# A hybrid encoder layer on one core: the first blocks, the token blocks and the convolution issue in written order, the conditioning is formed by quarters of the channels, h is made without GpSimd, and the staging tiles are fixed

## The chip, the cores and the metric

The kernel runs on one core of a Trainium2 chip. The metric is the device time of one execution in microseconds (us). The engines are TensorE (PE; its weight loads are listed apart as PEld), VectorE (DVE), ScalarE (ACT), GpSimd (POOL) and SyncE (SP, which here only issues transfers). Each engine works through a queue of its own in order. Transfers are issued from the queues of SP, ACT and POOL and run on 16 DMA engines.

## The reference

One layer with 2048 tokens of 1024 channels, all in float32:

```python
c_act = silu(c)
shift, scale, gate = split(c_act @ w_ada + b_ada, 3)      # the conditioning
h = rmsnorm(x, norm_w) * (1 + scale) + shift
proj = h @ w_in + b_in       # na_q, na_k, na_v, na_z, ml_q, ml_k, ml_v, ml_o, ml_z (512 columns each), 16 gate columns
na  = neighbourhood_attention(na_q, na_k, na_v, rpb) * silu(na_z)      # 32 x 64 grid, windows of 8 x 16, bias table rpb
mq, mk = silu(short_conv(ml_q, ml_k))                                  # 5 taps over the tokens
ml  = groupnorm((mlstm(mq, mk, ml_v) + mlstm_backward(...)) * sigmoid(ml_o)) * silu(ml_z)
out = rmsnorm(x + gate * (concat(na, ml) @ w_out), final_norm_w)
```

## The kernel before, in words

The product of two float32 matrices is made of three faster products: each operand is split into a high part (rounded) and a low part (the rest), and PE adds high x high, high x low and low x high. So h is kept as `hhi` and `hlo`, and a weight block as `whi` and `wlo`. A weight block is 256 columns of `w_in`; two slots, a and b, hold the block in use and the next one. A block comes in two halves (`raw0`, `raw1`); ACT copies a half into the high part and GpSimd subtracts for the low one (`load_w`).

The program runs in this order.

- **Start** (`start`). x comes in 16 tiles of 128 tokens, four to a group g (0 to 3). `prep_x` squares the four tiles on ACT, takes the reciprocal root on DVE (for group 0 on GpSimd) and scales the tiles. The conditioning is formed on DVE: for shift and scale, each of the eight row tiles of `w_ada` is multiplied by a column of silu(c) and added to `acc`, 512 columns at a time (`ada_tile`); PE then adds over the partitions with a column of ones (`columns`), and the results `gT` (scale) and `shT` (shift) are one number per channel. PE turns x into channel order (`turned`), and ACT and GpSimd, or ACT, DVE and GpSimd, make `hhi` and `hlo` for each of the eight channel tiles k (`first_h`, `scaled` and `shifted`, `make_h`).
- **Token blocks 0 and 1** (`vo_group`): values and output gate of two mLSTM heads, interleaved with the making of h for groups 1 to 3. A group is four token tiles of 24 matmuls each. In `vo_first` the four tiles are done side by side, so that they can begin when the first channels of h are there. Each result leaves PSUM (four tiles `pp`) by a DVE addition of the bias into a staging tile (`stvo`), ACT takes the sigmoid of the gate columns, and the tile is stored to `d_ck`. There are two staging tiles in turn. A store is put aside (`defer`) and issued on SP's queue when the next group ends (`flush`).
- **Token blocks 2 to 5** (`tok_blocks`): the other two heads, and the attention's values (`nav_group`, staging tile `stv`, stored to `d_vna`). Beside them runs a chain of small steps, one per token tile: the gate sums (`gate_chain`), then 16 groups of decays (`decays`): rows of `d_mneg` are loaded into one of two tiles `dec`, GpSimd adds a mask, ACT takes eight exponentials, and the result is stored to `d_ck`. Table entries for the attention's bias are filled (`table_fills`) and then spread by small DRAM to DRAM transfers (`tables_columns`, 48 of them, and `tables_rows`, 72).
- **Convolution** (`conv_blocks`): four blocks with the channels on the partitions, 32 tiles of 24 matmuls with 512 columns (`pc`); DVE does the five taps, ACT the SiLU (`acc`), and the keys are also turned by PE (`kt`) and stored through the staging tiles (`stk`).
- **Behind that**: the mLSTM passes, beside which the remaining projections run (`pq`), and the attention with the output projection.

Before the change the order of the instructions on each engine up to the attention is set by a scheduler, which takes a program order and moves instructions by estimated costs; only the attention is under `with tc.manual_schedule():`, in which instructions are issued as written. `rsqrt` is three Newton rounds of four operations (three where it is one column) behind two integer operations.

Of the kernel before, what the change touches and what calls it, by code (L numbers as in the profile page):

```python
# [15 lines left out]
P = 128  # L16
D = 1024
# [41 lines left out]
class Kernel:  # L59
# [73 lines left out]
    def phase1(self):  # L133
# [12 lines left out]
        self.stages = [self.qst, self.pool(r1a, "stage", bufs=1, side="right")]  # L146
# [17 lines left out]
        self.start(left)  # L164
        xs.close()

        self.tok_blocks(self.pool(toks, "chain", bufs=1, side="right"))
        toks.close()

        cvs = ExitStack()  # L170
        cvp = self.pool(cvs, "cvp", bufs=1, side="right")
        self.conv_blocks(cvp)
        cvs.close()
# [6 lines left out]
    def stage_tile(self, name):  # L180
        self.stages.reverse()
        return self.stages[1].tile([P, 1032], F32, tag="st", name=name).rearrange("p (o c) -> p o c", o=4)

    def load_w(self, blk, slot, halves=(0, 1)):
        nc = self.nc
        hi, lo = self.wslot[slot]
        for half in halves:
            raw = self.raw.tile([P, 4, 256], F32, tag=f"raw{half}", name=f"raw_{blk}_{half}")
            nc.sync.dma_start(raw, self.w_main[blk, :, 4 * half : 4 * half + 4, :])
            ks = slice(4 * half, 4 * half + 4)  # L190
            nc.scalar.activation(hi[:, ks, :256], raw, AF.Copy)
            nc.gpsimd.tensor_tensor(lo[:, ks, :256], raw, hi[:, ks, :256].bitcast(F32), ALU.subtract)

    def start(self, left):
        nc = self.nc
# [9 lines left out]
        xt = {}  # L205

        def load_x(tt):
            pool = early if tt // 4 == 2 else xp
            t = pool.tile([P, D], F32, tag="x", bufs=4, name=f"x_{tt}")
            nc.sync.dma_start(t, self.x[tt * P : (tt + 1) * P, :])  # L210
            xt[tt] = t

        def prep_x(tts):
            n = len(tts)
            ssq = xp.tile([P, n], F32, tag=f"ssq{n}", bufs=2, name=f"ssq_{tts[0]}")
            rst = xp.tile([P, n], F32, tag=f"rst{n}", bufs=2, name=f"rst_{tts[0]}")
            for i, tt in enumerate(tts):
                junk = xp.tile([P, D], mybir.dt.bfloat16, tag="junk", bufs=1, name=f"junk_{tt}")
                nc.scalar.activation(junk, xt[tt], AF.Square, accum_out=ssq[:, i : i + 1])
            nc.vector.tensor_scalar(ssq, ssq, 1.0 / D, EPS, ALU.mult, ALU.add)  # L220
            self.rsqrt(xp, rst, ssq, f"x{tts[0]}", nc.gpsimd if tts[0] == 0 else None)
            for i, tt in enumerate(tts):
                if tt < 4:
                    nc.scalar.activation(xt[tt], xt[tt], AF.Copy, scale=rst[:, i : i + 1])
                else:
                    nc.vector.tensor_scalar(xt[tt], xt[tt], rst[:, i : i + 1], None, ALU.mult)

        def ada_tile(part, q, kt):
            w = ada.tile([P, GT], F32, tag="wada", bufs=7, name=f"wada_{part}_{q}_{kt}")
            c0 = part * D + q * GT  # L230
            nc.sync.dma_start(w, self.w_ada[kt * P : (kt + 1) * P, c0 : c0 + GT])
            a = acc[:, c0 : c0 + GT]
            if kt == 0:
                nc.vector.tensor_scalar(a, w, cact[:, kt : kt + 1], None, ALU.mult)
            else:
                nc.vector.scalar_tensor_tensor(a, w, cact[:, kt : kt + 1], a, ALU.mult, ALU.add)
# [53 lines left out]
        for tt in range(4):  # L290
            load_x(tt)
# [1330 lines left out]
```

## Time and profile before

| | |
|---|---|
| times of three runs | 1407.24, 1409.82, 1413.92 us, median 1409.82 |
| the profiled execution | 1409.69 us, span 1407.8 us, mean granted clock 0.983 |
| PE busy | 1316.7 us (94%), 8052 matmuls |
| DVE busy | 834.7 us (59%) |
| ACT busy | 529.7 us (38%) |
| GpSimd busy | 284.5 us (20%) |
| DMA | 264.7 MB, 188 GB/s on average |

A line of a group names the source line, the engine, the operation, out<-in, the shapes, the count, and behind the bar the busy time in us, the mean of one in ns, the idle time of the engine before it and what ended that. A line of the timeline begins with start and duration in us. A line of a stretch has its bounds, its length, the busy us of PE, PEld, DVE, ACT and POOL with their instruction counts, the granted TensorE clock, the DMA share and GB/s. A line of waits is who waited, for whom, us in total, how often, and the longest. A busy PE is not a PE at its peak, since a slower clock counts as busy.

### The profile page before, as it was taken

How to read it: one execution, taken by the hardware profiler on the slowest of the kernel's cores; microseconds unless marked ns; L12 is line 12 of the kernel's file. 1: busy time of each engine (PE TensorE's matmuls, PEld its weight loads, DVE VectorE, ACT ScalarE, POOL GpSimd, SP SyncE). 2: the span in 40 equal slices, each digit the busy share in tenths (PEclk: the TensorE clock that was granted, in tenths of full speed). 3: DMA queues.
4: the chain of work that ended last, by engine and by line, in shares of the span. 5: the costliest groups of instructions: out<-in, count | busy, mean ns of one | idle time of the engine just before them, and what ended most of it. 6: DMA issues, size and time to landing. Idle time of an engine off the chain costs nothing. (4 is left out here: it accounts for less than half of the span.)

```text
span 1407.8 us, 23381 instructions
## 1 busy us (share of the span) xinstructions
PE 1316.7 (94%) x8052; PEld 1127.7 (80%) x8052; DVE 834.7 (59%) x2565; ACT 529.7 (38%) x1131; POOL 284.5 (20%) x309
## 2 busy tenths in 40 slices
PE   3989998898999999999999998999989999999996
PEld 2889998888887787788878786788867888888885
DVE  6683423211355569156757777877637777777674
ACT  4642344523222323113323313323336555555551
POOL 4353221424101010001212002212112211112111
PEclk9999999999999999999999999999999999999998
DMA  9798448777467675555666777946598897776862
GB/s 319 225 297 202 121 125 213 190 184 204 117 116 208 143 186 163 161 166 150 196 190 212 238 225 214 232 127 180 145 275 223 197 222 169 197 192 173 190 159 75
DMA packets 273036, 264.73 MB, mean 188 GB/s; under 512 B 33498, under 2 KB 233818, under 8 KB 272918
## 3 DMA queue, kind: packets, MB, share of 16 engines
q1 hardware_dynamic: 181486, 187.17, 50.3%
q0 software_dynamic: 21408, 38.05, 11.0%
q10 hardware_dynamic: 70024, 38.02, 9.6%
q8 instruction: 64, 1.05, 0.3%
q14 instruction: 54, 0.44, 0.1%
HBM read 178.62 MB, written 92.72 MB: 193 GB/s over the span
## 5 line engine op out<-in xcount | busy, mean ns | idle before, releaser
L861 PE MATMUL pq<-hhi,whi_a 128*128 128x512 f32 x512 | 211.6, 413 | 0.8 <-ACT u L769 0.8
L861 PE MATMUL pq<-hhi,wlo_a 128*128 128x512 f32 x512 | 211.4, 413 | 0.3 <-DVE wlo_a L838 0.3
L861 PE MATMUL pq<-hlo,whi_a 128*128 128x512 f32 x512 | 211.3, 413 | 0.0
L1342 ACT ACTIVATE pbuf<-pbuf,mn 128x480 f32<-128x480 f32 (+5 forms) x128 | 76.4, 598 | 115.3 <-DVE mn L1341 108.9
L861 PEld LDWEIGHTS pq<-hhi,whi_a 128*128 128x128 f32 x512 | 98.3, 192 | 19.4 <-ACT u L769 1.2
L861 PEld LDWEIGHTS pq<-hhi,wlo_a 128*128 128x128 f32 x512 | 98.2, 192 | 19.0 <-DVE wlo_a L838 0.8
L861 PEld LDWEIGHTS pq<-hlo,whi_a 128*128 128x128 f32 x512 | 98.3, 192 | 17.9
L1341 DVE CUSTOM_DVE_ANT_0 pbuf<-pS,tab 128x480 f32<-128x480 f32 (+5 forms) x128 | 65.2, 541 | 37.3 <-DMA tab<-d_t 20.1
L1415 PE MATMUL y<-hhi,whi_a 128*128 128x512 f32 x256 | 84.7, 400 | 0.7 <-ACT whi_a L1388 0.7
L1415 PE MATMUL y<-hhi,wlo_a 128*128 128x512 f32 x256 | 84.3, 399 | 0.0
L835 POOL TENSOR_TENSOR wlo_a<-rawq,whi_a 128x1024 fp32r<-128x1024 f32 x20 | 48.3, 2417 | 167.0 <-ACT whi_a L834 52.4
L425 PE MATMUL pvo<-whi_b,hhi 128*128 128x256 f32 x256 | 74.7, 292 | 7.5 <-DVE stvo L495 7.5
L1106 POOL TENSOR_TENSOR hm<-hm,ck 128x128 f32<-128x128 f32 x64 | 26.4, 413 | 266.5 <-DVE hm L1105 190.7
L1087 ACT ACTIVATE num<-px,gtile 128x129 f32<-128x129 f32 x120 | 38.2, 364 | 96.8 <-PE px L1082 79.9
L426 PE MATMUL pvo<-wlo_b,hhi 128*128 128x256 f32 x256 | 73.7, 288 | 0.0
L427 PE MATMUL pvo<-whi_b,hlo 128*128 128x256 f32 x256 | 73.5, 287 | 0.0
L1014 DVE TENSOR_SCALAR wv<-kv,gtile 128x129 f32<-128x129 f32 x120 | 38.5, 328 | 58.4 <-PE dc L1030 30.4
L495 DVE TENSOR_TENSOR stvo<-pvo,brow 128x256 f32<-128x256 f32 x64 | 26.6, 421 | 73.4 <-PE pvo L427 59.5
L710 ACT ACTIVATE dec<-dec,gtile 128x128 f32<-128x128 f32 x128 | 42.1, 392 | 74.0 <-POOL dec L706 64.8
L460 DVE TENSOR_TENSOR stv<-pv,brow 128x256 f32<-128x256 f32 x32 | 12.5, 421 | 89.2 <-DMA d_vna<-stv 41.6
L1363 PE MATMUL pT<-ident,pbuf 128*128 128x128 f32 (+2 forms) x416 | 59.8, 283 | 2.8 <-DVE pbuf L1353 2.8
L1378 PE MATMUL pO<-pt,v 128*64 128x128 f32 (+3 forms) x832 | 61.0, 280 | 1.3 <-ACT pt L1365 0.8
(295 smaller groups left out, 3578.0 us busy)
## 6 DMA issues: line engine op xcount, KB each, us to landing
ck<-d_ck SPq DMA_DIRECT2D x64, 384.5 KB
kv<-d_ck SPq DMA_DIRECT2D x120, 128.5 KB
rawq<-in_w_main_dram SPq DMA_DIRECT2D x30, 512.0 KB
raw<-in_w_main_dram SPq DMA_DIRECT2D x20, 512.0 KB
d_ck<-stvo SPq DMA_DIRECT2D x16, 514.0 KB
x<-in_x_dram SPq DMA_DIRECT2D x16, 512.0 KB
wada<-in_w_ada_dram SPq DMA_DIRECT2D x32, 256.0 KB
dec<-d_mneg SPq DMA_DIRECT2D x32, 256.0 KB
```

The costliest lines, as they stand in the source:

```text
L425: nc.tensor.matmul(ps, lhi(k), rhi(k), start=(k == 0), stop=False)
L426: nc.tensor.matmul(ps, lhi(k), rlo(k), start=False, stop=False)
L427: nc.tensor.matmul(ps, llo(k), rhi(k), start=False, stop=(k == KT - 1))
L710: nc.scalar.activation(t[:, d, o, :], t[:, d, o, :], AF.Exp, bias=self.cols["g"][:, d, h, c : c + 1])
L835: nc.gpsimd.tensor_tensor(lo[:, :, cs], raw, hi[:, :, cs].bitcast(F32), ALU.subtract)
L861: nc.tensor.matmul(patch_ps(ps) if patch else ps, w, self.htok(h, g, k, patch), start=(k == 0 and n == 0), stop=(k == KT - 1 and n == 2))
L1014: nc.vector.tensor_scalar(wv, tiles[d, i][:, 128:257], self.cols["w"][:, d, h, c : c + 1], None, ALU.mult)
L1341: nc.vector.tensor_tensor_reduce(pt[:, :nk], ps, tabs[place[u]][j][:, :nk], 1.0, 3e38, ALU.add, ALU.min, mn)
L1342: nc.scalar.activation(pt[:, :nk], pt[:, :nk], AF.Exp, bias=mn, scale=-1.0, accum_out=sums[:, j : j + 1])
L1363: nc.tensor.transpose(ps[:cs, i, :], pts[j][:, i * cs : (i + 1) * cs], self.ident)
L1378: nc.tensor.matmul(po[j * HD : (j + 1) * HD, :], v[:n, h * HD : (h + 1) * HD], pt[j][:n, i, :], start=(i == 0), stop=(i == nch - 1))
L1415: nc.tensor.matmul(y, m[:, k, :], w[k][:, cs], start=(k == 4 and n == 0), stop=(k == 3 and n == 2))
```

## The change

Everything from the start to the end of the convolution is put under the manual schedule, so the order is the written one, and the written order is changed with it. The conditioning is formed in quarters of 256 channels: for each quarter scale, then shift, then the two channel tiles of h, then their matmuls side by side. h is made by ACT (scaled, then high part) and DVE (low part); the root is taken on DVE for every group. Block 1's first group is also done side by side. The two staging tiles are made once, with their column of ones written once. Stores of the values and of the convolution go out on ACT's queue at once, those of `d_vna` on SP's; decay loads, table columns and table rows go to GpSimd's queue, the last two a few at a time. Weight halves are loaded and split at given places. The square root has one operation less in each round. The core of the diff:

```diff
-        self.stages = [self.qst, self.pool(r1a, "stage", bufs=1, side="right")]
+        stage = self.pool(r1a, "stage", bufs=1, side="right")
+        self.stages = [pl.tile([P, 1032], F32, tag="st", name=f"st{i}").rearrange("p (o c) -> p o c", o=4) for i, pl in enumerate((self.qst, stage))]
+        for st in self.stages:
+            nc.gpsimd.memset(st[:, :, 128:129], 1.0)
...
-        self.start(left)
...
+        with tc.manual_schedule():
+            self.start(left)
...
+            self.tok_blocks(self.pool(toks, "chain", bufs=1, side="right"))
...
+            self.conv_blocks(cvp)
...
+        def make_h(g, k):
+            turned(g, k)
+            scaled(g, k)
+            shifted(g, k)
...
+        def modulation(part, q):
+            c0 = part * D + q * 256
+            a = acc[:, c0 : c0 + 256]
+            for j in range(4):
+                n = 8 * q + 4 * (1 - part) + j
+                w = wada.pop(n)
+                for i in range(2):
+                    c = cact[:, 2 * j + i : 2 * j + i + 1]
+                    if j == 0 and i == 0:
+                        nc.vector.tensor_scalar(a, w[:, i, :], c, None, ALU.mult)
+                    else:
+                        nc.vector.scalar_tensor_tensor(a, w[:, i, :], c, a, ALU.mult, ALU.add)
+                load_ada(n + 7)
+            ps = self.sp.tile([P, 2], F32, tag="sp", name=f"mod_{part}_{q}")
+            for j in range(2):
+                nc.tensor.matmul(ps[:, j : j + 1], a[:, j * P : (j + 1) * P], self.ones[:, 0:1], start=True, stop=True)
...
+        prep_x(0)
+        for k in range(3):
+            turned(0, k)
+        first = self.side_by_side(0, 0)
+        for q in range(4):
...
+            modulation(1, q)
+            for k in (2 * q, 2 * q + 1):
+                scaled(0, k)
+                if k + 3 < KT:
+                    turned(0, k + 3)
...
+            modulation(0, q)
+            for k in (2 * q, 2 * q + 1):
+                shifted(0, k)
+                next(first)
...
+        self.vo_tiles(0, 0)
+        second = self.side_by_side(1, 0)
+        for k in range(KT):
+            if k == 3:
+                prep_x(1)
+            next(second)
...
+        self.chain = steps(2, ((0, 1, 2), (3, 4, 5), (6, 7)), lambda: prep_x(2))
+        self.vo_group(1, 1, 1)
...
-        self.flush()
-        dst = self.d_vna[g * GT : (g + 1) * GT, c0 : c0 + 256].rearrange("(o p) c -> p o c", p=P)
-        self.defer(lambda: nc.sync.dma_start(dst, st[:, :, :256]))
+        nc.sync.dma_start(self.d_vna[g * GT : (g + 1) * GT, c0 : c0 + 256].rearrange("(o p) c -> p o c", p=P), st[:, :, :256])
...
+    def vo_store(self, h, g):
+        nc, st = self.nc, self.stages[1]
+        nc.scalar.activation(st[:, :, 129:257], st[:, :, 129:257], AF.Sigmoid)
+        nc.scalar.dma_start(self.d_ck[h, 4 * g : 4 * g + 4, :, 128:385].rearrange("o p c -> p o c"), st[:, :, 0:257])
...
-            nc.sync.dma_start(self.d_e[ct][:, i, :, start - k0 : start - k0 + 16], self.d_rneg[:, :, dx : dx + 16])
+            self.nc.gpsimd.dma_start(self.d_e[ct][:, i, :, start - k0 : start - k0 + 16], self.d_rneg[:, :, dx : dx + 16])
+            yield
...
+        columns = itertools.chain(*(self.tables_columns(ct) for ct in range(3)))
+        self.chain = self.beside(self.chain, columns)
...
+                if g < 2:
+                    self.split_w(raws[g], (blk + 1) % 2, g)
+                next(self.fills, None)
...
-                nc.sync.dma_start(flat[:, d * 512 : (d + 1) * 512], src.broadcast_to([P, 512]))
+                nc.gpsimd.dma_start(flat[:, d * 512 : (d + 1) * 512], src.broadcast_to([P, 512]))
...
             nc.gpsimd.tensor_tensor(t, t, mask.unsqueeze(2).broadcast_to([P, 2, 4, CH]), ALU.add)
+            if n + 1 < len(groups):
+                load(n + 1)
+            yield
...
+                    for _ in range(3):
+                        next(rows, None)  
...
-        nc.sync.dma_start(dst, acc.rearrange("p (c t) -> p c t", t=CH))
+        nc.scalar.dma_start(dst, acc.rearrange("p (c t) -> p c t", t=CH))
...
-            eng.tensor_scalar(t, t, -0.5, 1.5, ALU.mult, ALU.add)
-            eng.tensor_tensor(y, y, t, ALU.mult)
+            nc.vector.scalar_tensor_tensor(y, t, 1.5, y, ALU.add, ALU.mult)
```

How the order moves is shown at three places. The first is DVE's queue in the first block, before: `acc` are the conditioning steps with 512 columns, `ssq` and `rst` belong to the root of group 0.

```order
L234 TENSOR_SCALAR acc<-wada_0_0_197,cact 128x512
L220 TENSOR_SCALAR ssq_167<-ssq_167 128x4
L1182 TENSOR_SCALAR rst_168<-ssq_167 128x4
L1183 TENSOR_SCALAR rst_168<-rst_168 128x4
L236 SCALAR_TENSOR_TENSOR acc<-wada_0_1_200,cact,acc 128x512
L236 SCALAR_TENSOR_TENSOR acc<-wada_0_2_203,cact,acc 128x512
```

The steps run on from there, all 32, and the small operations of the root are on GpSimd. Now DVE's queue from the first scale (`gT`) to the second quarter; `mod` is what PE has added over the partitions, `hlo` the low part of h for the channel tiles 0 and 1:

```order
L294 SCALAR_TENSOR_TENSOR gT<-mod_0_256,bada 128x2
L295 TENSOR_TENSOR gT<-gT,nw 128x2
L285 TENSOR_SCALAR acc<-wada_0_0_187,cact 128x256
L287 SCALAR_TENSOR_TENSOR acc<-wada_0_0_187,cact,acc 128x256
L287 SCALAR_TENSOR_TENSOR acc<-wada_0_1_189,cact,acc 128x256 x2
L287 SCALAR_TENSOR_TENSOR acc<-wada_0_2_191,cact,acc 128x256 x2
L287 SCALAR_TENSOR_TENSOR acc<-wada_0_3_242,cact,acc 128x256 x2
L297 TENSOR_TENSOR shT<-mod_0_291,bada 128x2
L251 SCALAR_TENSOR_TENSOR hlo_105<-hg_0_261,shT,hhi_102 128x512
L251 SCALAR_TENSOR_TENSOR hlo_105<-hg_1_268,shT,hhi_102 128x512
L285 TENSOR_SCALAR acc<-wada_1_0_246,cact 128x256
```

The steps of a quarter now stand behind operations that wait for PE (`gT`, `shT`) and for ACT (`hlo`).

The second place is ACT's queue where the x tiles of group 2 are squared (`junk`), before; `stvo_0_597` is the staging tile of group 1 of one block, `hhi_103` the high part of h for group 1, `hhi_104` that for group 2.

```order
L499 ACTIVATE stvo_0_597<-stvo_0_597 128x4x128
L285 ACTIVATE hhi_103<-tp_6_713,shT,gT 128x512
L285 ACTIVATE hhi_103<-tp_7_722,shT,gT 128x512
L219 ACTIVATE junk_1213,ssq_1211<-x_1095 128x1024
L219 ACTIVATE junk_1215,ssq_1211<-x_1097 128x1024
L219 ACTIVATE junk_1217,ssq_1211<-x_1099 128x1024
L219 ACTIVATE junk_1219,ssq_1211<-x_1101 128x1024
L285 ACTIVATE hhi_104<-tp_0_907,shT,gT 128x512
L285 ACTIVATE hhi_104<-tp_1_916,shT,gT 128x512
L499 ACTIVATE stvo_1_867<-stvo_1_867 128x4x128
```

And now; `st_123` is the fixed staging tile with group 1 of block 0:

```order
L493 ACTIVATE st_123<-st_123 128x4x128
L494 DMA d_ck<-st_123 128x4x257
L229 ACTIVATE junk_0_949,ssq_947<-x_572 128x1024
L229 ACTIVATE junk_1_951,ssq_947<-x_574 128x1024
L229 ACTIVATE junk_2_953,ssq_947<-x_576 128x1024
L229 ACTIVATE junk_3_955,ssq_947<-x_578 128x1024
L234 ACTIVATE x_574<-x_574,rst_948 128x1024
L234 ACTIVATE x_578<-x_578,rst_948 128x1024
L245 ACTIVATE hg_0_1006<-tp_0_1001,gT 128x512
L250 ACTIVATE hhi_104<-hg_0_1006,shT 128x512
```

The sigmoid of block 0's group 1 moved from behind the squares of group 2, where the next sigmoid stood, to ahead of them, and two of the four x tiles are now scaled by ACT behind them.

The third place is SP's queue in block 4, before: `stv` are the staging tiles, `dec` the decay rows, `d_t` table rows.

```order
L189 DMA raw_1_3278<-in_w_main_dram 128x1024
L547 DMA d_t_75<-d_e_72 8x16x192
L698 DMA dec_0_2969<-d_mneg 128x512 x2
L464 DMA d_vna<-stv_0_2752 128x4x256
L698 DMA dec_1_3064<-d_mneg 128x512 x2
L547 DMA d_t_75<-d_e_72 8x16x192 x2
L464 DMA d_vna<-stv_1_2877 128x4x256
L698 DMA dec_2_3159<-d_mneg 128x512 x2
L698 DMA dec_3_3254<-d_mneg 128x512 x2
```

And now, SP's queue at the same stores (`wide` are rows for the output gate's sums):

```order
L469 DMA brow_138<-in_b_row_dram 128x256
L401 DMA wide<-in_w_ada_dram 128x1024 x2
L466 DMA d_vna<-st_123 128x4x256
L401 DMA wide<-in_w_ada_dram 128x1024
L466 DMA d_vna<-st_124 128x4x256
L466 DMA d_vna<-st_123 128x4x256
L415 DMA wide<-in_b_gate_dram 1x1024
L466 DMA d_vna<-st_124 128x4x256
```

The decay loads and the table transfers left SP's queue, and a store stands at the end of its own group.

More of the change, by code (lines that the diff above doesn't have):

```diff
@@ L204, in start @@
         nw = ada.tile([P, KT], F32, name="nw")
[L205 to L219, printed above, removed]
+        rg = xp.tile([P, KT, 16], F32, name="rg")
```

375 lines of the change are left out of this document (170 added, 205 removed).

## The prediction

> **What bounds the kernel now.** I read the busy shares first (PE works 1316.7 of 1407.8 us), then one table of stretches, then PE's waits in the part that the change rewrites. The stretches are cut at the first transpose, the ends of the first block of matmuls, of both first weight blocks, of weight blocks 2 to 5, and of the convolution; all behind 556.9 is left as it is but for the square root. The table's columns are busy us (and instructions) of the five engines, the granted clock, and the DMA engines.
>
> ```profile
> 0.00:18.70 18.70, 0.00 (x0) 0.00 (x0) 6.87 (x15) 7.27 (x12) 6.83 (x21) 1.00 0.91 331
> 18.70:53.30 34.60, 27.90 (x160) 25.83 (x161) 27.66 (x34) 18.34 (x28) 20.08 (x16) 0.95 0.73 238
> 53.30:155.80 102.50, 96.39 (x772) 94.16 (x771) 57.15 (x131) 42.03 (x62) 37.48 (x35) 0.98 0.92 235
> 155.80:362.90 207.10, 193.18 (x1557) 189.49 (x1556) 48.31 (x112) 80.67 (x169) 58.50 (x33) 0.97 0.69 175
> 362.90:556.90 194.00, 187.86 (x833) 151.18 (x831) 118.62 (x227) 56.29 (x85) 20.02 (x8) 0.99 0.65 158
> 556.90:1407.80 850.90, 811.39 (x4736) 667.02 (x4736) 576.13 (x2051) 325.13 (x778) 141.56 (x197) 0.99 0.70 187
> ```
>
> PE is idle 18.7, 6.7, 6.1, 13.9, 6.1 and 39.5 us there. So the rewritten part can give back some 50 us at most, and only where its order doesn't bring waits of its own. Who ended those waits (us in total, times, longest), up to 600 us:
>
> ```profile
> PE tp L258 <- ACT x L224: 18.7, 1, 18.7
> PE pvo L425 <- DVE stvo L495: 7.5, 3, 3.6
> PE pv L425 <- DVE stv L460: 6.4, 2, 4.7
> PE kt L815 <- ACT acc_k L805: 6.1, 5, 2.8
> PE tp L283 <- DVE h L287: 4.6, 4, 2.1
> PE pvo L478 <- ACT hhi L265: 4.4, 1, 4.4
> ```
>
> The 13.9 us of blocks 2 to 5 are DVE's additions into the staging tile, which came late. The next lines tell why: DVE waited for the store of that tile, and the store stood on SP's queue behind loads of decay rows that waited for their buffer.
>
> ```profile
> DVE stv L460 <- DMA d_vna<-stv: 41.6, 4, 15.1
> SPq L698 <- DMA d_ck<-dec: 64.9, 18, 9.1
> ```
>
> **Term 1, the first block (to 53.3 us).** x is squared as before; the last sum is there at 10.04. The square root leaves GpSimd for DVE: 13 small operations instead of 15, 0.20 apart by the next rows, so 12.65. DVE and ACT then scale two x tiles each (0.68 and 1.07 apart): 14.0 and 14.8. So the transposes start 4 us sooner than at 18.7.
>
> ```profile
> 9.86 0.18 ACT L219 ACTIVATION_READ_ACCUMULATOR junk<-x 128x1 f32 x1
> 60.30 0.16 DVE L1189 TENSOR_TENSOR nwt_x<-rst 128x4 f32<-128x4 f32 x1
> 60.50 0.16 DVE L1190 TENSOR_TENSOR nwt_x<-nwt_x,ssq 128x4 f32<-128x4 f32 x1
> 62.90 2.73 DVE L226 TENSOR_SCALAR x<-x,rst 128x1024 f32<-128x1024 f32 x4
> 17.52 4.27 ACT L224 ACTIVATE x<-x,rst 128x1024 f32<-128x1024 f32 x4 [7.48 <-POOL rst L1192]
> ```
>
> Then the conditioning. Before, 32 steps of 512 columns run ahead of the matmuls. Now 64 steps of 256 columns stand on DVE in eight portions, with the subtractions of h between them, so each portion waits for the one before to be used up. The price of a step:
>
> ```profile
> 416.87 2.73 DVE L804 SCALAR_TENSOR_TENSOR acc_k<-u,cw,acc_k 128x512 f32<-128x512 f32 x4
> 10.56 5.47 DVE L236 SCALAR_TENSOR_TENSOR acc<-wada,cact,acc 128x512 f32<-128x512 f32 x7
> L838 DVE SCALAR_TENSOR_TENSOR wlo_a<-rawq,whi_a 128x1024 fp32r<-128x1024 f32 x10 | 12.2, 1224 | 5.4 <-ACT whi_a L837 4.4 <-PE pq L861 0.8
> L1074 DVE SCALAR_TENSOR_TENSOR ck<-a,ck 128x256 f32<-128x256 f32 x64 | 26.9, 420 | 0.9 <-PE a L1069 0.7
> ```
>
> A chain of 512-column steps runs 0.66 apart ((2.73-0.75)/3), and 0.79 where each waits for a load ((5.47-0.75)/6). 512 columns more cost 1.22-0.75 = 0.48, so 256 fewer save 0.24: 0.42, and 0.55 on every second step, which waits for a load. A portion of eight is 0.3 + 4 x 0.55 + 3 x 0.42 = 3.8. Ends: 3.0 if the saving is in proportion to the columns (0.33 and 0.46), 5.3 if a step costs what 512 columns do. I take 3.8, since the one row of 256 columns lasts 0.42.
>
> ```profile
> 38.17 0.95 PE L242 MATMUL mod<-ones,acc 128*128 128x1 f32 x8
> 29.95 0.78 ACT L265 ACTIVATE hhi<-tp,shT,gT 128x512 fp32r<-128x512 f32 x1 [3.37 <-POOL shT L246]
> 45.33 2.74 DVE L276 SCALAR_TENSOR_TENSOR hlo<-hg,shT,hhi 128x512 fp32r<-128x512 f32 x4 [1.22 <-ACT hhi L275]
> 24.56 8.73 DVE L236 SCALAR_TENSOR_TENSOR acc<-wada,cact,acc 128x512 f32<-128x512 f32 x7
> 26.11 2.33 POOL L192 TENSOR_TENSOR wlo_a<-raw,whi_a 128x1024 fp32r<-128x1024 f32 x1
> 48.00:50.00 2.00, 2.00 (x10) 2.00 (x10) 0.70 (x2) 0.96 (x2) 1.84 (x1) 0.50 0.84 153
> ```
>
> A quarter is two portions (7.6), two trips to PE and back (two of the eight matmuls of 0.95, with both hand-overs 0.5 each), three small operations (0.6), ACT's upper part (0.78) and two subtractions (0.69 each): 11.4. Four of them from 14.0 end at 59.4. GpSimd splits three weight halves meanwhile: the seven steps beside such a split took 8.73 where 5.47 was usual, so up to 3.3 a time; I take 1.6, since DVE is itself waiting for part of it: +4.8. Behind the last subtraction PE has some 12 matmuls left, 0.126 each by the tile price of the next part, or 0.25 at the half clock that the last row grants after short waits: +2.3. The first block ends at 66.5, against 53.3: **+13.2** (+1.5 with 3.0 us portions and no collision, +25 with 5.3 us ones).
>
> **Term 2, the rest of weight blocks 0 and 1.** GpSimd's 24 subtractions and DVE's h go; ACT makes one more pass and DVE subtracts. Per k that is at most 1.6 us of ACT (twice 0.78) and 0.7 of DVE beside twelve matmuls and four transposes, some 2 us of PE: hidden. The squares of x are not: ACT's queue has them behind the sigmoid of the group before.
>
> ```profile
> 205.28 1.28 ACT L499 ACT_TABLE_LOAD   x1
> 206.57 0.64 ACT L499 ACTIVATE stvo<-stvo 128x512 f32<-128x512 f32 x1
> 6.31 1.06 ACT L219 ACTIVATE junk<-x 128x1024 bf16<-128x1024 f32 x1 [0.21 <-DMA x<-in_x_dram]
> 7.59 1.06 ACT L219 ACTIVATE junk<-x 128x1024 bf16<-128x1024 f32 x1
> 256.09 0.43 DVE L495 TENSOR_TENSOR stvo<-pvo,brow 128x256 f32<-128x256 f32 x1 [3.73 <-PE pvo L427]
> 258.93 0.42 DVE L495 TENSOR_TENSOR stvo<-pvo,brow 128x256 f32<-128x256 f32 x1 [2.42 <-PE pvo L427]
> ```
>
> From the end of a group: additions 0.6, sigmoid 0.64 (once with a table load of 1.28), four squares 1.28 apart, square root 2.6, scaling 2.1: ready after 11.1 us, the first time 12.4. A token tile takes 2.84. For x tiles 4 to 7 PE has four tiles to do (11.4): it waits 1.0, and about 1.0 more for the first h. For tiles 8 to 11 it has two (5.7): it waits **5.4**. Tiles 12 to 15 have a whole group ahead: no wait. 7.4 us against 6.1 before; and the long one slows the clock, as the stretch around a 3.6 us gap shows (0.83 over ten us, so 1.7 us):
>
> ```profile
> 245.00:255.00 10.00, 6.41 (x41) 6.21 (x41) 3.64 (x5) 4.36 (x10) 2.44 (x2) 0.83 0.70 209
> 560.00:600.00 40.00, 40.00 (x170) 31.81 (x169) 7.23 (x14) 7.94 (x11) 2.40 (x1) 1.00 0.51 152
> ```
>
> Half of that was lost before too, by the 0.98 of that stretch: **+2.2**. The Trainium skill, TensorE: Matmul & The Clock Gate (Part 1), says that the clock halves after an idle window of about 3.4 us and returns after as long a busy one; by it, and 1.7 us for 3.4 us at half clock, the term is the same.
>
> **Term 3, weight blocks 2 to 5.** Stores no longer wait for the next group, the decay loads and the table columns leave SP's queue for GpSimd's, and the other stores go to ACT's. A store is then issued when its group ends, and its tile is wanted a group (11.4 us) later, with four PSUM tiles before PE feels it. 64 tiles x 2.84 = 181.8; the 21 other matmuls some 4, and one wait of some 1.2 for an addition and four small DVE copies (0.42 + 4 x 0.20) behind which the order puts a small product: 187 against 207.1. I leave one us: **-19**. What this asks of GpSimd: per decay group (three tiles, 8.5 us) one mask addition, two loads and three columns, and on average 0.9 of a weight split.
>
> ```profile
> L706 POOL TENSOR_TENSOR dec<-dec,mask 128x1024 f32<-128x1024 f32 x16 | 38.5, 2405 | 88.8 <-DMA dec<-d_mneg 59.4 <-DMA raw<-in_w_main_dram 13.5 <-DMA d_t<-d_e 10.9
> L1271 POOL DMA_DIRECT2D v<-d_vna x40: 626/680/907, 1019.4 to 1347.3; - x40
> 149.96 7.88 SPq L524 DMA_DIRECT2D d_e<-d_rneg  x8
> ```
>
> No row has a DRAM-to-DRAM issue on GpSimd. By its loads 0.68, by the same columns on SP 0.99 (7.88/8): 3.3 + 5 x 0.68 = 6.7 or 8.2 us of the 8.5. I take the lower, the same engine's: hidden.
>
> **Term 4, the convolution.** 48 stores and the 72 table rows leave SP; ACT issues the stores (0.4 us each beside 1.4 to 2.0 us of work per 6.1 us tile: covered), GpSimd three rows per tile. The transposes stand two tiles behind the activation they read, so the 6.1 us of kt waits go. 768 matmuls at 40/170 = 0.235 and 64 transposes: 189 against 194.0: **-5** (0 if the waits come back).
>
> **Term 5, the square root.** One operation of four goes from each round; in the rest of the kernel DVE is free for a third of the time, so I count nothing, and 0.4 in the last patch's chain: **-0.4**. The weights, fills and fixed staging tiles cost the same as before.
>
> Sum: 13.2 + 2.2 - 19 - 5 - 0.4 = -9.0. Against the profiled execution's 1409.7 (its span and 1.9 around it) that is 1400.7, say 1400; the median of the runs is 1409.8, the same.
>
> **The rivals.**
> A, the first block eats the gain. With steps of 0.50 and 0.62 a portion is 4.3, a quarter 12.4, the block ends at 71 and, with full collisions (3 x 3.3), at 76: 4 to 9 more than the forecast, 1405 to 1410, no change. For it: DVE's chain has no second thing to do. Against: the 256-column row.
> B, the first block costs little. Portions of 3.0 and no collision give +1.5, in all -21: 1389. For it: GpSimd's rows collide with DVE at only three places.
> C, slower: GpSimd's queue becomes the bound of blocks 2 to 5. It decides from 1.04 us an issue ((8.5-3.3)/5); at 1.7 a group takes 11.8, 3.3 too much for 16 groups, 53 us, of which a staging turn and four PSUM tiles (20) hide the first part: +33 in place of nothing, 1434. ACT's exponentials wait for GpSimd, the sigmoids for these, then stores, additions, PE. For it only the columns' 0.99 on SP; against it GpSimd's longest of 40 issues, 0.91, with DVE two thirds busy. The Trainium skill, SBUF — State Buffer (SBUF: two separate sides), states this mechanism: GpSimd can't write descriptors while a DVE operation holds the port that they share, 0.62 us alone and 3.1 behind a long copy. By its figure (an estimate) a group would take 3.3 + 15.5 = 19 us, and blocks 2 to 5 would lose over 100; the 0.91 speaks against it, and DVE is busy only 48 of 207 us here.
> D, the order brings nothing: SP's queue still holds stores back, behind loads of the gate's weights that wait for DVE (blocks 4 and 5 alone). Then half of term 3 is lost: 1410.
>
> **How the numbers follow.** The forecast (1396 to 1404) has 0.40, A and D together 0.25, B 0.20, C 0.12, and 5.3 us portions (1413) 0.03. What a measurement can tell from no change is about 0.5%, 7 us: faster is below 1402.8. The forecast gives 0.32 of its share to that, B all of it: 0.52; the same gets 0.08 + 0.25 + 0.03 = 0.36; slower 0.12. The range holds B, A and D: 1388 to 1413.
>
> **What would show it.** The first token block's last matmul near 66 us, DVE there without a pause and PE half idle; PE's one long wait (5.4) before the transposes of x tiles 8 to 11; no wait of PE for stvo, stv or kt of more than a us; blocks 2 to 5 in 187 us; mean GpSimd issues below 1 us. Wrong it would be by portions of another length than 3.8, by GpSimd issues over 1 us, or by a pass of decays that holds ACT.

## The result and the profile after

The changed kernel took 1455.17 us (median of four runs, 1449.52 to 1457.96) against 1408.99 for the kernel before: ratio 1.032, 95% interval 1.028 to 1.036. It is slower by 3.2%, where 1400 was forecast. In a later set of runs both kernels were some 1% faster, and the ratio was 1.030 (1.026 to 1.033). The experiments belong to that time, so they are compared with the profiles of that set, called "before, second" (span 1387.0 us) and "after, second" (1432.4 us).

The same table of stretches as in the prediction, now of the changed kernel, cut at the first transpose, the ends of the first block, of blocks 0 and 1, of blocks 2 to 5, and of the convolution (columns: bounds, length, busy us of PE, PEld, DVE, ACT, POOL with instruction counts, granted clock, DMA share, GB/s):

```profile
0.00:13.43 13.43, 0.00 (x0) 0.03 (x1) 3.07 (x17) 6.99 (x11) 0.77 (x8) 1.00 0.86 302
13.43:75.50 62.07, 37.40 (x162) 33.00 (x163) 45.25 (x92) 16.96 (x24) 10.61 (x6) 0.73 0.67 211
75.50:177.70 102.20, 96.61 (x770) 95.16 (x770) 40.16 (x111) 59.04 (x87) 4.77 (x2) 0.96 0.39 107
177.70:387.10 209.40, 192.96 (x1556) 188.65 (x1554) 50.06 (x114) 71.50 (x145) 97.28 (x101) 0.97 0.82 193
387.10:591.80 204.70, 189.59 (x832) 153.45 (x832) 127.58 (x223) 64.55 (x107) 68.64 (x87) 0.96 0.68 175
591.80:1456.20 864.40, 815.25 (x4737) 668.81 (x4736) 562.74 (x1994) 327.47 (x781) 143.81 (x198) 0.98 0.71 186
```

The first block ends at 75.5 instead of 53.3: +22.2. Blocks 0 and 1: -0.3. Blocks 2 to 5: +2.3. Convolution: +10.7. Behind it: +13.5. Together the 48.4 us between the two spans. Only blocks 0 and 1 came out near the forecast (+2.2). Of the 48.4 us, PE's own busy time is 15.1 (1331.8 against 1316.7, with the same 8052 matmuls), and 9.5 of that lie in the first block (37.4 against 27.9): the granted clock is 0.73 there, and 0.96 to 0.97 where PE waits later. The rest is idle time.

Who ended PE's waits from block 2 to the first projection (us in total, times, longest):

```profile
PE pv L429 <- DVE st L464: 13.0, 3, 6.3
PE kt L836 <- ACT acc_k L826: 9.5, 1, 9.5
PE pq L882 <- ACT u L789: 7.4, 1, 7.4
PE pc L429 <- DVE st L464: 5.7, 1, 5.7
```

The waits for the staging tiles did not go. Those of blocks 2 and 3 did (7.5 us before `pvo`), but those of blocks 4 and 5 grew from 6.4 to 13.0 (`pv`), and one of 5.7 stands before the convolution (`pc`). One long wait before `kt` took the place of five short ones, and a new one stands before the first projection. One step behind, DVE's own waits, then those of SP's queue:

```profile
DVE st L464 <- DMA d_ck<-st: 30.1, 2, 15.3
DVE st L464 <- DMA d_vna<-st: 27.9, 2, 15.8
```

```profile
SPq L466 <- DMA d_ck<-dec: 43.4, 4, 16.5
...
SPq L401 <- DVE st L464: 25.8, 2, 15.9
```

DVE still waits for stores of the staging tiles, and SP's stores (L466) wait for stores of decays on ACT's queue. Nothing in the source asks for that: the additions and the store have nothing to do with decays. The built program tells why. It gives the transfers of SP and ACT eight semaphores (counters that report a landing) in turn, and seven of the eight L466 stores wait for the transfer that had their semaphore before. For four of them that is a decay store on ACT's queue, so SP stands still until it has landed. Two of the seven, the first of which waits for a decay store and the second for a store of SP's own:

```
107 L466 DMA d_vna<-st_123 128x4x256 [waits DMAHW4_49,DVE_49]
...
111 L466 DMA d_vna<-st_124 128x4x256 [waits DMAHW4_49,DVE_49]
```

### The profile page after: what moved, and what is told of

It is laid out like the page before. It is cut to its first block, busy times and chain, and to the rows that moved or that the text cites. A ratio compares the mean times of both kernels' runs of the same rounds, so it can differ in the third digit from the quotient of the medians.

```text
span 1456.2 us, 23316 instructions
## 1 busy us (share of the span) xinstructions
PE 1331.8 (91%) x8052; PEld 1139.1 (78%) x8052; DVE 828.9 (57%) x2548; ACT 546.5 (38%) x1153; POOL 325.9 (22%) x400
## 3 DMA queue, kind: packets, MB, share of 16 engines
q0 software_dynamic: 30496, 54.74, 16.5%
q10 hardware_dynamic: 103816, 59.03, 15.1%
## 5 line engine op out<-in xcount | busy, mean ns | idle before, releaser
L1362 ACT ACTIVATE pbuf<-pbuf,mn 128x480 f32<-128x480 f32 (+5 forms) x128 | 76.4, 598 | 113.9 <-DVE mn L1361 106.0
L487 DVE TENSOR_TENSOR st<-pvo,brow 128x256 f32<-128x256 f32 x64 | 26.6, 423 | 89.8 <-PE pvo L431 61.4
L464 DVE TENSOR_TENSOR st<-pv,brow 128x256 f32<-128x256 f32 x32 | 12.6, 421 | 92.6 <-PE pv L431 34.6
L429 PE MATMUL pvo<-whi_b,hhi 128*128 128x256 f32 x224 | 64.4, 288 | 0.4 <-DVE gates L489 0.4
L430 PE MATMUL pvo<-wlo_b,hhi 128*128 128x256 f32 x224 | 63.6, 284 | 0.0
L431 PE MATMUL pvo<-whi_b,hlo 128*128 128x256 f32 x224 | 63.6, 284 | 0.0
## 6 DMA issues: line engine op xcount, KB each, us to landing
d_ck<-st ACTq DMA_DIRECT2D x16, 514.0 KB, 10.1
```

What stands on the lines that cost most here:

```text
L429: nc.tensor.matmul(ps, lhi(k), rhi(k), start=(k == 0), stop=False)
L430: nc.tensor.matmul(ps, lhi(k), rlo(k), start=False, stop=False)
L431: nc.tensor.matmul(ps, llo(k), rhi(k), start=False, stop=(k == KT - 1))
L1362: nc.scalar.activation(pt[:, :nk], pt[:, :nk], AF.Exp, bias=mn, scale=-1.0, accum_out=sums[:, j : j + 1])
```

## Experiments

The stages of all runs, in us, cut at the last matmul of each; one profiled execution each. The stage behind the convolution differs by 4 to 10 us between two executions of the same kernel (850.9 and 846.5 before, 864.4 and 854.4 after). The ratio is that of the timed runs. Of the single changes below only e3_dec3 and e5_halves have a ratio whose interval lies below that of the changed kernel; for the others the stages and waits are what speaks.

| kernel | first block | 0 and 1 | 2 to 5 | conv | behind | ratio (95%) |
|---|---|---|---|---|---|---|
| before, second | 54.1 | 99.9 | 196.2 | 190.3 | 846.5 | 1 |
| after, second | 74.8 | 101.2 | 201.7 | 200.3 | 854.4 | 1.030 (1.026-1.033) |
| u1_start | 75.2 | 109.2 | 196.6 | 198.3 | 860.5 | 1.034 (1.031-1.038) |
| u2_rest | 62.4 | 99.2 | 202.6 | 200.6 | 866.2 | 1.024 (1.021-1.026) |
| e1_first | 66.2 | 101.6 | 205.8 | 201.7 | 864.1 | 1.027 (1.023-1.031) |
| e2_fills | 75.1 | 101.2 | 191.2 | 201.7 | 859.8 | 1.027 (1.024-1.030) |
| e3_dec3 | 75.4 | 101.4 | 197.5 | 196.3 | 857.2 | 1.024 (1.022-1.026) |
| e4_silu | 76.4 | 101.5 | 202.2 | 198.1 | 853.7 | 1.026 (1.023-1.029) |
| e5_halves | 63.3 | 101.4 | 199.6 | 200.9 | 857.6 | 1.021 (1.019-1.023) |
| d1_sp | 76.4 | 101.8 | 210.4 | 185.4 | 856.0 | 1.028 (1.024-1.031) |
| c2_all | 62.0 | 102.1 | 192.1 | 187.2 | 852.5 | 1.003 (1.001-1.005) |
| c3_all | 61.0 | 100.5 | 193.6 | 191.4 | 852.5 | 1.000 (0.998-1.002) |
| c4_all | 56.7 | 99.2 | 196.5 | 186.5 | 850.0 | 0.997 (0.995-0.999) |

**The base again.** after2 is the changed kernel, before2 the kernel before.

> The changed kernel again, beside the runs of the experiments: the base that their stages are compared with. Theory: the ratio to the kernel before stays at 1.028 to 1.036, and the stages that the experiments did not touch (blocks 0 and 1, the attention) agree with theirs within a us; rival: block 4 and the projections differ by 5 us and more from run to run, and the smaller gains of the experiments are not theirs.

> The kernel before again, for its stages beside those of the experiments. Theory: the 12 us by which it is faster here than in the profile shown lie in blocks 2 to 5 and the first block, where transfers and waits set the time; rival: the whole span is shorter by the granted clock.

The ratio held, and blocks 0 and 1 agree with the experiments within 1 us apart from u1 and u2. But block 4 was 56.6 instead of 60.7 and the projections 514.0 instead of 524.7, so differences of that size there are not read as effects. Of the 20.8 us by which the kernel before was shorter here (1407.8 to 1387.0), 10.9 lie in blocks 2 to 5 (207.1 to 196.2) and none in the first block. PE's busy time, at a clock of 0.988 instead of 0.983, gives 7.5 of the 20.8; in blocks 2 to 5 PE's idle time fell from 13.9 to 7.0 us. So half of the waits that the forecast wanted to win back are not there in another execution.

**Half of the change undone.**

```diff
 # u1_start: blocks 2 to 5 and the convolution by the scheduler
         with tc.manual_schedule():
             self.start(left)
             xs.close()
-            self.tok_blocks(...)
+        self.tok_blocks(...)
...
 # u2_rest: the start by the scheduler
-        with tc.manual_schedule():
-            self.start(left)
+        self.start(left)
+        with tc.manual_schedule():
             self.tok_blocks(...)
```

> The start and token blocks 0 and 1 keep the written order; token blocks 2 to 5 and the convolution go back to the scheduler, with their code as changed. Theory 'order': of the 46 us, the parts lost in blocks 2 to 5 (2.4), the convolution (10.7) and behind it (13.5) come from the written order, which puts work behind waits on ACT, SP and DVE; then they go, and the time is 1425 to 1432, or as low as 1412 if blocks 2 to 5 also gain what was forecast. Rival 'traffic': the table transfers and decay loads on GpSimd's queue cost it, whatever the order; then 1450 to 1460. The first block ends at 75 us in both.

> The start and token blocks 0 and 1 (code as changed, quarters included) go back to the scheduler; blocks 2 to 5 and the convolution keep the written order. Theory 'order': the first block's 22 us come from DVE standing behind PE and ACT between the portions, which a scheduler moves apart; it ends at 55 to 62 us, and the time is 1436 to 1443. Rival 'quarters': 64 steps of 256 columns cost what they cost in any order; the block ends at 70 us or later, 1450 to 1456.

u1 did not get faster (1.034 against 1.030), which by the ratio is what the rival said; its range in us, like that of the theory, was worked out from the slower first set. The stages speak for a mixture. Blocks 2 to 5 take 196.6, as before the change, but the scheduler put a DVE operation on `bcol` ahead of a root, DVE waited 13.9 us for that transfer, and blocks 0 and 1 lost 8 us. The loss of the convolution (198.3) is not undone by the order alone. u2 bears its theory out at the upper edge: with the same quarters, a scheduler ends the first block at 62.4.

**The first block.**

```diff
 # e1_first: DVE's next portion ahead of what is done with the last one
+            ps = modulation(part, q)
+            while lows: low(lows.pop(0))
+            finish(*last)
+            ... scaled / high of the portion before
 # e5_halves: the same with 512 columns
-        pieces = [(part, q, j) for q in range(4) for part in (1, 0) for j in range(4)]
+        pieces = [(part, q, j) for q in range(2) for part in (1, 0) for j in range(KT)]
```

> The changed kernel, with DVE's conditioning one portion ahead of what is done with the one before (the scale, the shift and the low part of h are taken after the next portion). Theory 'hand-overs': DVE's waits between portions, some 2.8 us per quarter, go: the last subtraction moves from 70.6 to about 61, the first block ends at 65 to 66 us instead of 75.25, and the time is 1445 to 1447. Rival 'loads': the transfers of w_ada set the pace; the block ends at 73 us or later and the time stays at 1453 to 1457.

> The changed kernel with the conditioning in halves of 512 columns, 32 steps as before the change, still in written order, DVE's portions ahead of what is done with them. Theory 'step price': 64 steps of 256 columns cost 0.51 each, 32 of 512 some 0.68, so DVE saves 10 us beside the hand-overs; then the loads of w_ada bound it, and the first block ends at 52 to 58 us instead of 75.25; ratio to the kernel before 1.018 to 1.022. Rival 'written order': in any written order DVE and PE stand behind each other; the block ends above 62 us, ratio above 1.024.

A quarter of the changed kernel on DVE, from its timeline (start, duration, then what it waited for in brackets):

```profile
28.77 0.35 DVE L285 TENSOR_SCALAR acc<-wada,cact 128x256 f32<-128x256 f32 x1
29.15 3.61 DVE L287 SCALAR_TENSOR_TENSOR acc<-wada,cact,acc 128x256 f32<-128x256 f32 x7
33.52 0.16 DVE L294 SCALAR_TENSOR_TENSOR gT<-mod,bada 128x2 f32<-128x2 f32 x1 [0.76 <-PE mod L291]
...
33.80 0.35 DVE L285 TENSOR_SCALAR acc<-wada,cact 128x256 f32<-128x256 f32 x1
34.18 3.61 DVE L287 SCALAR_TENSOR_TENSOR acc<-wada,cact,acc 128x256 f32<-128x256 f32 x7
38.95 0.16 DVE L297 TENSOR_TENSOR shT<-mod,bada 128x2 f32<-128x2 f32 x1 [1.17 <-PE mod L291]
39.96 1.41 DVE L251 SCALAR_TENSOR_TENSOR hlo<-hg,shT,hhi 128x512 fp32r<-128x512 f32 x2 [0.85 <-ACT hhi L250]
41.29 0.35 DVE L285 TENSOR_SCALAR acc<-wada,cact 128x256 f32<-128x256 f32 x1
```

A portion is 4.0 us, and three waits of 0.76, 1.17 and 0.85 stand in each quarter. In e1 the portions follow each other, and the block ends 8.6 us earlier: the hand-overs, as their theory said; the loads do not set the pace. The timed runs gained only 0.003, inside the intervals, since the stages behind the first block were longer in the profiled execution. Halves (e5) bring the ratio that was expected, but the block ends at 63.3, better than 66.2 and not at 52 to 58: the price of a step was not the whole rest (c4 below).

**The table fills.** Of the nine transfers that fill the bias tables (`d_t`<-`big`, 1.0 to 1.9 MB each), the kernel before issued all from 60 to 110 us, the changed one from 104 to 261 us.

```diff
 # e2_fills: two behind the first block, three behind the second group, two behind the third
+        self.fills = self.table_fills()
+        next(self.fills)
+        next(self.fills)
         second = self.side_by_side(1, 0)
...
-        self.fills = self.table_fills()
+        for _ in range(3):
+            next(self.fills)
```

> The changed kernel, with seven of the nine table fills issued in token blocks 0 and 1 (two behind the first block, three behind the second group, two behind the third) instead of three. Theory 'full DMA engines': the stores of the staging tiles land 10 to 15 us late since the DMA share is above 1 from 220 to 290 us; the share falls below 0.9 there, the stores land within 8 us, PE's waits of 13 us before pv go, and the time is 1440 to 1446. Rival 'decay loop': a decay group takes 10.9 us since its two buffers go around mask, exponentials, store and load, and everything queued behind it waits; the time stays within 5 us of 1455.

The stretch from 220 to 300 us, first of the kernel after, then of after, second, and last of e2_fills (the DMA share is the last figure but one):

```profile
220.00:300.00 80.00, 73.67 (x605) 73.31 (x604) 16.00 (x34) 29.73 (x56) 32.25 (x33) 0.96 1.06 234
```

```profile
220.00:300.00 80.00, 76.67 (x633) 76.25 (x631) 17.07 (x32) 32.49 (x63) 34.35 (x33) 0.98 0.99 248
```

```profile
220.00:300.00 80.00, 79.76 (x674) 79.55 (x673) 20.48 (x38) 35.17 (x68) 41.69 (x41) 1.00 0.75 201
```

With the fills out of it the DMA engines have room, stores to `d_ck` from 200 to 320 us land in 6.9 us (median; 8.7 in after, second; the longest 10.7 against 15.1), and PE is busy for 79.8 of the 80 us. PE's waits before `pv` fall to 0.2 us (6.8 in after, second, and 13.0 in the first profile), as the theory said. Blocks 2 to 5 take 191.2 instead of 201.7, in one execution each. The gain in time of 9 to 15 us did not come: the ratio fell by 0.003, inside the intervals, and in the profile the stage behind the convolution was 5.4 us longer, which is within what it varies by. So the mechanism is shown, and its worth is not resolved. A decay group still took 10.7 us here, so the rival's loop is there as well.

**The decays.**

```diff
 # e3_dec3: a third buffer, loads two groups ahead
-            flat = pool.tile([P, D], F32, tag=("wgate", "gacc")[n % 2], ...)
+            flat = self.wide[:, D:] if n % 3 == 2 else pool.tile([P, D], F32, tag=("wgate", "gacc")[n % 3], ...)
-            if n + 1 < len(groups): load(n + 1)
+            if n + 2 < len(groups): load(n + 2)
 # d1_sp: decay loads on SP's queue, two buffers
-                nc.gpsimd.dma_start(flat[...], ...)
+                nc.sync.dma_start(flat[...], ...)
```

> The changed kernel with a third buffer for the decay rows (half of wide; the gate's sums then have one buffer instead of two), so that a load is issued two groups ahead. Theory 'decay loop': with two buffers a group costs half of load, mask, exponentials, store and landing, 11 us (178 us for 16), where the order gives it 8.5; SP's and ACT's transfers stand behind these stores, and the staging tiles behind them. With three buffers the 16 groups take 140 to 150 us and end with block 5; the waits before kt (9.5) and pc (5.7) go, and the ratio to the kernel before falls from 1.032 to 1.012 to 1.020 (20 to 28 us less). Rival 'full DMA engines': the loads and stores land as late as before, since the transfers as a whole are too many there; block 4 stays above 57 us and the ratio above 1.025.

> The changed kernel with the decay loads back on SP's queue, two buffers as there. Theory 'two buffers': a group goes through load, mask, exponentials, store and landing at half of 21 to 22 us whichever queue issues the load; it stays at 10 to 11 us and the ratio within 0.005 of the changed kernel's. Rival 'GpSimd's queue': the loads come late because GpSimd stands at columns and splits before them; on SP a group takes 9.2 as before the change, the ratio falls by 0.010 or more.

The stores of the decays, first and last issue, in after (second), before (second), d1_sp and e3_dec3 (where a third of the tiles has another name):

```profile
L735 ACTq DMA_DIRECT2D d_ck<-dec x32: 366/366/367, 235.2 to 398.2; - x32
```

```profile
L712 ACTq DMA_DIRECT2D d_ck<-dec x32: 366/366/670, 209.1 to 342.7; - x32
```

```profile
L735 ACTq DMA_DIRECT2D d_ck<-dec x32: 366/366/410, 245.8 to 397.6; - x32
```

```profile
L738 ACTq DMA_DIRECT2D d_ck<-dec x22: 366/366/393, 241.5 to 377.7; - x22
```

From the first to the last store are 15 groups and 1.7 us: 10.8 us a group in the changed kernel (the last ends 21 us behind block 5), 8.8 before, 10.0 with the loads on SP, 9.0 with three buffers. So three buffers do to the pace what their theory said, block 4 takes 46.7 us instead of 56.6, and PE's wait before `kt` (10.7) is gone. Loads on SP do it less, and the ratio stays, as the theory of two buffers had it. But the ratio of e3, 1.024, missed its 1.012 to 1.020: block 5 is 5.6 us longer (54.6), and PE waits 7.8 before `pc`. These three lines of e3 (PE, DVE and SP's queue around 370 us) tell why:

```profile
PE pc L428 <- DVE st L463: 7.8, 1, 7.8
DVE st L463 <- DMA d_vna<-st: 18.2, 1, 18.2
SPq L465 <- DMA d_ck<-dec: 13.7, 1, 13.7
```

An SP store of a staging tile again waits for a decay store on ACT's queue, DVE for that store, and PE for DVE. No run takes this wait away by itself. d1 gains 15 us in the convolution and loses 9 in blocks 2 to 5, where SP is again held up by the loads.

The kernel before held 8.8 with two buffers too, and the traces say where it saves. From the issue of a group's loads to the next load into the same buffer it took 17.3 us (median), half of which is 8.6; the changed kernel (second) took 20.2. The difference lies between the store and the next load: 4.9 against 8.2 us. What makes that part longer was not tried. The DMA share there (0.69 against 0.80) does not explain it alone, since in blocks 2 to 5 of e2_fills it is 0.63 and a group takes 10.7.

**The convolution.**

```diff
 # e4_silu
+        yield
         nc.scalar.activation(acc, acc, AF.Silu, ...)
```

> The changed kernel with the convolution's SiLU issued one tile later on ACT. Theory 'ring': a tile's result leaves PSUM on ACT behind the SiLU of the tile before, which waits for DVE's taps, which wait for the result before: 0.7 + 0.2 + 3.6 + 0.7 + 0.4 = 5.6 us a tile, as much as PE's 5.7, so what is late at the start of the convolution (9.5 us) stays late to its end and is paid again as PE's wait of 7.4 before the first pq. Without the ring the lag is made up: the wait of 7.4 falls below 1, the projections behind it gain 8 to 10 us, the ratio to the kernel before is 1.024 to 1.027. Rival 'lag elsewhere': DVE (4.6 us a tile) or the transfers hold the tiles; the wait stays above 5 us, and the ratio within 0.003 of 1.032.

ACT in the convolution, after (second), then e4_silu:

```profile
552.14 0.73 ACT L826 ACTIVATE acc_q<-acc_q,cb 128x512 f32<-128x512 f32 x1 [3.77 <-DVE acc_q L825]
552.89 0.37 ACTq L829 DMA_DIRECT2D d_ck<-acc_q  x1
553.30 0.69 ACT L789 ACTIVATE u<-pc,bcol 128x512 f32<-128x512 f32 x1 [0.44 <-ACT acc_q L826]
```

```profile
550.30 0.69 ACT L789 ACTIVATE u<-pc,bcol 128x512 f32<-128x512 f32 x1 [4.28 <-PE pc L431]
550.89 0.71 ACT L827 ACTIVATE acc_q<-acc_q,cb 128x512 f32<-128x512 f32 x1
```

In the written order a PSUM result leaves only when the SiLU before it is done, and that waits for DVE; in e4 the result leaves when PE has it. PE's wait before the first projection, after (second) and e4_silu:

```profile
PE pq L882 <- ACT u L789: 5.4, 1, 5.4
```

```profile
PE pq L882 <- ACT u L789: 0.8, 1, 0.8
```

The wait before `kt` stays (10.8), but its lag is made up by the end of the convolution: the ring is shown. Its price is not resolved. The convolution is 2.2 us shorter, the projections behind it take 514.0 in both where 8 to 10 us less were expected, and the two ratios' intervals overlap.

**All causes together.** c2 joins e2 to e5. c3 adds three moves; c4 keeps two of them and, instead of the third, gives the root of group 0 back to GpSimd and its scaling to ACT.

```diff
 # c3 and c4: the squares of x tiles 8 to 11 ahead of the sigmoid; a step between two copies of the gate chain and their matmuls
+        squares(2)
         self.vo_tiles(0, 1)
...
 # c4: group 0
-            self.rsqrt(xp, rst, ssq, f"x{g}")
+            self.rsqrt(xp, rst, ssq, f"x{g}", None if g else nc.gpsimd)
```

> All four together: halves in the first block, seven table fills in blocks 0 and 1, a third buffer for the decay rows, SiLU one tile later. If the four causes are separate and together are the change's loss, the stages are 55 (first block), 101, 186 to 190 (blocks 2 to 5), 190 to 194 (convolution), 512 to 517 and 340: 1384 to 1397 against 1408 before, ratio 0.982 to 0.992. If they are one lag that moves from place to place, the gains don't add, and the ratio stays above 1.000.

> The four together as before, and three moves more: DVE's first portion of the conditioning ahead of the root of group 0; the squares of x tiles 8 to 11 ahead of the sigmoid of block 0's second group; a step of the gate chain between two copies on DVE and the matmuls that read them. If each takes away the wait that stands at its place (4 to 5 us in the first block; the wait of 4.0 and its half clock in blocks 0 and 1; 1.6 and its half clock in block 2), the stages are 57.5, 97, 48 to 49 (block 2), the rest as before: 1381 to 1386 us where the four alone had 1395.9, ratio 0.992 to 0.996. If the waits only move, the ratio stays at 1.001 to 1.005.

> The four together, the squares of x tiles 8 to 11 early, the gate chain's extra step (with one step of the decays dropped for it), and in the first block the root of group 0 on GpSimd and its scaling on ACT, as before the change. Theory 'DVE's queue': what the first block still costs over the kernel before (61 to 62 us against 54) is the root and the scaling, 4.1 us of DVE and 3 us of waits around them that stand ahead of the conditioning; it ends at 56 to 58, blocks 0 and 1 take 100, block 2 48.5, the whole 1386 to 1390 and the ratio 0.994 to 0.998. Rival 'written order': the portions' waits for PE and GpSimd's splits hold the block at 60 us or later, and the ratio is 0.999 to 1.003.

The four together missed what was expected: the median of the timed runs is 1402.6 us (the profile's span alone, 1395.9, is inside 1384 to 1397), and the ratio of 1.003 is above the range, on the rival's side. Part of that is the kernel before, which takes 1396 here and not the 1408 from which the ratio was worked out; part is the first block, at 62.0 and not 55. Blocks 2 to 5 (192.1) and the convolution (187.2) come near what the forecast had for the change itself. That the gains don't add is not borne out: apart, e2, e3, e4 and e5 lower the ratio by 0.003, 0.006, 0.003 and 0.009, together 0.021, and c2 lowers it by 0.026. So these four causes are nearly all of the 3%.

c3 missed too, at 1.000. Its extra step made the decays end some 3.7 us later, counted from the start of block 2, and block 5 and the convolution gave back what block 2 gained (4.6 and 4.2 for 3.6). c4's first block and convolution (two of its stretches):

```profile
0.00:56.70 56.70, 29.54 (x161) 27.27 (x162) 34.64 (x56) 25.98 (x36) 17.48 (x26) 0.94 0.87 306
...
352.40:538.90 186.50, 185.69 (x833) 150.61 (x832) 131.41 (x231) 57.80 (x84) 56.21 (x70) 1.00 0.64 175
```

The first block ends at 56.7 instead of 62.0 in c2 (PE's clock is 0.94 in both, where the changed kernel has 0.79). So the root and the scaling on DVE were most of what c2 still lost there, as the theory of DVE's queue had it. With 0.997 (0.995 to 0.999) c4 has just made good the loss: it is 0.3% below the kernel before, a difference that is clear of the interval but small. Its blocks 2 to 5 take 196.5, no less than before the change, so the gain that was forecast there is not in it: block 2 gained 3.6 us over c2, and block 4 lost 7.5.

## Why the prediction was wrong

- **Term 1 (+13.2; measured +22.2, and +20.7 in the second pair).** The mechanism was right: DVE is the chain, and PE was busy 37 of 62 us. Four sizes were low. A portion took 4.0 instead of 3.8 (1.6 in eight). The hand-overs of a quarter took 2.8 (0.76, 1.17, 0.85), which with its small steps made 12.5 instead of 11.4 (some 3 more in four quarters). A GpSimd split cost a portion 2.1 instead of 1.6 (5.64 to 5.83 for 3.61, three times). And behind the last subtraction PE had 20 matmuls and 4.7 us left, not 12 and 2.3, since its last burst runs at 0.227 us a matmul to the end of the block.
- **Term 2 (+2.2; -0.3 and +1.3).** Right in kind: PE's long wait before the transposes of x tiles 8 to 11 is there, 3.98 instead of 5.4 us; the waits of 1.0 before the others did not come.
- **Term 3 (-19; +2.3 and +5.5).** Two steps failed. "The weights, fills and fixed staging tiles cost the same as before": the fills moved by 40 to 150 us, most of the way into the blocks where decays, stores and gate weights run. With them moved back (e2) PE's waits before `pv` are gone, and blocks 2 to 5 were 10.5 us shorter in one execution each, which the timed runs do not resolve. And the decays were costed by GpSimd's busy time (6.7 of 8.5 us a group), not by the way of one buffer through mask, exponentials, store and load, with two landings in it: 2.4 + 3.7 + 7.6 + 1.2 + 5.8 = 20.7 for two groups, 10.3 each, by the durations and median landings of the second profile, against 10.8 measured. In this written order what came late stayed late, and so did what stood behind it on ACT's and SP's queues. Besides, the 13.9 us of waits that the term wanted to win back are only 7.0 in the second profile of the kernel before.
- **Term 4 (-5; +10.7 and +10.0).** That "the 6.1 us of kt waits go" failed: they became one wait of 9.5, since the decays ended 26 us (21 in the second pair) behind block 5 and the convolution's tiles wait for them; in e3 the decays end 3 us behind it, and the wait is gone. That the SiLU and the PSUM copies stand in a ring (0.7 + 0.2 + 3.6 + 0.7 + 0.4 = 5.6 us a tile, PE's own 5.7), so that a lag is never made up, was not seen.
- **Term 5 and all behind (-0.4; +13.5 and +7.9).** In the first pair the wait of 7.4 before the first projection and the slower PE behind it (3.9 us more busy time in this stage) are the larger part. In the second pair the wait is 5.4, and e4, which takes 4.6 of it away, leaves the stage 0.7 us shorter; so how much the wait is worth stays open. A wait of 2.5 for `qst`, which the kernel before has not, stays unexplained.
- **Rivals.** A (a dearer first block) came true in its size, but it was not alone. C named the losing side with the wrong mechanism: GpSimd's issues took 0.56 to 0.62 (medians of its three kinds), far below the 1.04 from which it decides. The Trainium skill, SBUF — State Buffer (SBUF: two separate sides), has 3.1 us for a transfer of GpSimd's queue beside a DVE copy; none of the 152 issues here came near it (the longest 0.81). D was half right: SP did hold stores back behind gate weights (25.8 us), and behind decays too, but its loss was taken as a lost gain only. Each rival was priced alone, and here several losses came together.

## What to carry to other kernels

When a scheduled stretch is written out by hand, list for each buffer the whole way around (load, work, store, two landings) and hold its time against the pace at which the order uses it; busy time of an engine says nothing about it. Then list every bulk transfer that the new order moves, also those that nothing waits for, and look at the DMA share of the place where they land. Within an engine's queue, put what frees a buffer of PE ahead of what waits for another engine.

## What was not expected of the hardware

Seven stores of 514 KB from 200 to 320 us landed in 8.6 to 15.1 us where the DMA share was 0.99 (after, second, 220 to 300 us), and in 3.5 to 10.5 us where it was 0.75 (e2_fills). A transfer on one queue waited up to 16.5 us for one on another, through a shared semaphore (argued from the program's list of waits and the trace, not tried by itself). In the first block PE worked in bursts of at most some 6 us between waits of up to 6.7, and its granted clock was 0.73 over 62 us; so 9.5 of the 22.2 us lost there are PE's own busy time.
